# One attention output norm per query block, the residual sum on GpSimd, and shorter one-column roots in a two-layer hybrid decoder step

## The chip, the cores and the metric

The kernel runs on one core of a Trainium2 chip. The metric is device time in microseconds (us) from launch to end; the time of a kernel is the median of its runs. The engines are TensorE (PE in the profile; PEld is its weight load), VectorE (DVE), ScalarE (ACT), GpSimd (POOL) and SyncE (SP), whose queue issues the DMAs here. Each engine runs its own instructions in a fixed order; they wait for each other by semaphores.

## The reference, cut to what matters

One inference step of two layers over 2048 prompt tokens and 64 sample tokens (8 rows of 8), width 1024. Each layer projects its modulated input into four branches: A (differential attention), B (spatial gate), C (convolution), D (gated recurrence). Each branch is multiplied by a SiLU gate, the four are joined and projected, and the residual update normalizes the result:

```python
p = probs(q1, k1) - lam * probs(q2, k2)          # softmax over the visible keys
o_a = einsum('bhqk,bkhd->bqhd', p, v)            # 4 heads of 64 value columns
o_a = _rms_norm(o_a, attn_norm_g[l]) * (1.0 - lam_init)
o_a = o_a * silu(ag)
mixed = concatenate([o_a, o_b, o_c, o_d], -1) @ w_out[l]
y = _layer_norm(ALPHA * x + gate[:, None, :] * mixed, ln_g[l], ln_b[l])
```

`_rms_norm` divides the 64 values of a head by the root of their mean square plus EPS; `_layer_norm` takes the mean and the variance (plus EPS) of a row of 1024. ALPHA is (2 x 2 layers)^0.25.

## The kernel before

A layer has two stages. The first makes the projections and the branches B, C and D and writes queries, keys, values, gates and the joined branches to DRAM. The second, the attention stage, runs `attention` and `out_tile` (lines 1489 to 1516) and is the one that the change touches. In the profile it lies at 1065 to 1640 us for the first layer and at 2590 us to the end for the second.

The attention works on query blocks of tiles of 128 tokens: blocks of 4, 4, 4, 2 and 2 tiles, so 5 per layer. For each block, `attention` (line 620) loops over the 4 heads: it loads the head's keys and queries, and for each tile `attn_probs` (line 653) makes the scores on TensorE into one of two PSUM buffers (L668), the negated row maximum on VectorE (L672), the exponential on ScalarE with its row sum (L676), and joins the two softmaxes without dividing by the sum of the first (L697, L702; small columns in L674 to L692). `attn_value` (line 705) transposes the probabilities (L715, L717) and multiplies with the values (L720) into one PSUM bank. The row sum l of the first softmax stays in the tile `ls`.

After the last tile of a head, `attn_value` goes on with the norm of that head (lines 726 to 747): copy out of PSUM, transpose, copy to `ot`, square (ScalarE), sum of squares over 64 columns (L737), mean square plus EPS times l squared (L738, L739, since the output is not divided by l), the root (L740, which calls `rsqrt`, line 174: L179 and L181 for the first estimate, then three Newton steps in L183, L189 and L190), the product with the root (L742) and the product with the norm's weights (L746 on GpSimd; L744 on VectorE in the last block). The head's 64 columns are then stored to the scratch tensor `cat`, except in the last block, where they stay in `act`. `rsqrt` runs on VectorE here: its `pool` argument is false. Each step is one instruction on columns as wide as the number of tiles (4 or 2).

`out_tile` (line 1313) makes one tile of 128 tokens of the layer's output: it loads `cat`, the gates and the other branches, multiplies (L1336 on GpSimd, L1342 on VectorE), splits the product in a high and a low part (L110 on ScalarE, L172 mostly on GpSimd), multiplies with the two parts of `w_out` in two halves of 512 columns (L1360 to L1362), and for each half multiplies by the adaLN gate (L1364), adds ALPHA times the old x (L1365) and takes the statistics (L1366), all on VectorE. Then come mean and variance (L1368), EPS (L1370), the one-column root (L1371), the affine step on ScalarE (L1376) and the two products and sums with the LayerNorm's weights (L1377, L1378), on GpSimd except in the last two tiles, and the store. The output tiles of a block are emitted after the attention of the next block; the last two tiles (`last`) follow their own block directly. With the sample there are 17 tiles per layer. x and the gated product share four buffers (tag `xs`).

The order of the work on each engine is not the order of the code. A planner arranges the instructions before the run from a simulated timeline and from priorities (`prio`, offsets in `KN`: the output tiles have -500, the probabilities 0), and SP's queue has the loads and stores in one order as well. On the chip that order is fixed. Buffers are tiles of pools: a tile with `bufs=1` can be written again only after all its readers are done.

Of the kernel before, what the change touches and what calls it, by code (L numbers as in the profile page):

```python
# [9 lines left out]
F32 = mybir.dt.float32  # L10
# [4 lines left out]
AF = mybir.ActivationFunctionType  # L15
# [9 lines left out]
P = 128  # L25
# [43 lines left out]
def hymba_step_kernel(  # L69
# [21 lines left out]
    # order, engines and buffers: P* offsets of priority, E* / L* / R* choice of engine, the others counts and orders  # L91
# [16 lines left out]
    def cpy(k, out, in_):  # L108
        """copy by ScalarE or VectorE"""
        (nc.vector.tensor_copy if KN[k] else nc.scalar.copy)(out, in_)  # L110
# [18 lines left out]
    # pools of the phase: PSUM banks of the projections, a second bank for transposes  # L129
# [4 lines left out]
    def nm(s):  # L134
        uid[0] += 1
        return f"{s}_{uid[0]}"
# [14 lines left out]
    def st(tag, dt=F32):  # L151
        """rows of 512 of the streams that run beside each other: zs slabs, ms branches, os input and output"""
        return stp.tile([P, 512], dt, tag=tag, name=nm(tag), bufs=NST[tag])

    # small columns: width by stream
    SW = dict(d=8, a=4, b=2, c=4, o=1, s=4, p=4)
# [17 lines left out]
    def rsqrt(v, M, n, who, pool=True):  # L174
        """1 / sqrt(v) in place for v [M, n] > 0: estimate from the exponent bits, three Newton steps."""
# [5 lines left out]
        eng.tensor_scalar(y.bitcast(I32), i, -1.0, float(0x5F3759DF), op0=ALU.mult, op1=ALU.add)  # L181
        for _ in range(3):
# [10 lines left out]
    def gate2(dst, t, x):  # L193
        """2 silu(x) = (tanh(x / 2) + 1) x, given t = tanh(x / 2)"""
        nc.vector.scalar_tensor_tensor(dst, t, 1.0, x, op0=ALU.add, op1=ALU.mult)  # L195

# [16 lines left out]
    # page indices: row = (layer * NPOOL + page) * 128 + partition  # L213
# [15 lines left out]
    # conditioning vectors, transposed  # L229
# [50 lines left out]
    def mod(l, Lx, part, mp, bank=None):  # L280
        """shift, 1 + scale or gate of the rows of c, features on partitions."""
        dst = (Lx.shT, Lx.sc1T, Lx.gT)[part]
        for half in range(2):
# [7 lines left out]
            # the four sums are added once features are on partitions  # L291
# [14 lines left out]
        if part == 2:  # L306
            for half in range(2):
# [4 lines left out]
                nc.vector.tensor_copy(row[0:9], ps[0:9])  # L312
                store(scr[l].gate[:, half * 512:(half + 1) * 512], row[0:9])

    def prep(l, Lx, hp):
        """small tensors of a layer; hp: those that only the first phase needs"""
# [19 lines left out]
        with tc.tile_pool(name=nm("prep"), reuse_waits="tile", bufs=1) as pp:  # L336
# [16 lines left out]
            # lower bound: cumulative softmax over the layers, without the first  # L353
# [18 lines left out]
            # head norms; A and D carry the 1/2 of their gate  # L372
# [4 lines left out]
            # lambda of the differential attention  # L377
# [11 lines left out]
            # convolution taps  # L389
# [7 lines left out]
            # 1/4: the halves of the swish and of the gate  # L397
# [3 lines left out]
            # spatial weights, lower triangle  # L401
# [10 lines left out]
            # 1/2 of the gate in the weights and in the bias  # L412
# [13 lines left out]
    # state kept between the groups of a layer  # L426
# [92 lines left out]
    def tok_pairs(g):  # L519
        """(first token column, global tile, number of tiles, rows, is sample)"""  # L520
# [23 lines left out]
    def mix(main, n, *fills):  # L544
        """main (about n steps) with each fill (generator, steps, share of main over which it is spread) in between"""
# [18 lines left out]
    # ================= A: differential attention =================  # L564
# [55 lines left out]
    def attention(l, t0, nt, Lx, ap, act=None):  # L620
        """nt tiles of queries from tile t0"""
# [8 lines left out]
        vst = pool.vst  # L630
        for hd in range(4):
# [11 lines left out]
            ls = smp.tile([P, 4], F32, tag="ls", name=nm("ls"), bufs=3)  # L643
            acc = None
            for j in range(nt):
                pm = prio(KN['PPB'] if t0 else KN['PPB'], attn_probs, t0 + j, qt[:, :, j * P:(j + 1) * P], kst, ls[:, j:j + 1], Lx, ap)
# [3 lines left out]
                prev = (lambda *a: lambda: attn_value(*a, Lx, l, ap))(t0 + j, pm, vst, acc, ls, j, nt, hd, act)  # L650
        prev()

    def attn_probs(qi, qt, kst, l1, Lx, ap):
        """p1 - lam (l1 / l2) p2, unnormalized; l1"""
# [6 lines left out]
        for m in range(2):  # L661
            pms = []
            for pc, n in enumerate(sizes):
# [7 lines left out]
                # negated running maximum  # L671
# [7 lines left out]
            if npc > 1:  # L679
                # factor of the first part, whose maximum may have been smaller  # L680
# [24 lines left out]
    def attn_value(qi, pm, vst, acc, ls, j4, nt, hd, act, Lx, l, ap):  # L705
        """values of even key tiles on the lower columns of the array, of odd ones on the upper"""
# [19 lines left out]
        asb = ap.o.tile([P, 512], F32, tag="asb", name=nm("asb"), bufs=1)  # L726
        cpy('EAS', asb[:, 0:nt * P], acc[:, 0:nt * P])
        # transposed, the two halves of the columns added
# [3 lines left out]
        ot = ap.o.tile([P, 4, 64], F32, tag="ot", name=nm("ot"), bufs=1)[:, 0:nt]  # L732
        nc.scalar.copy(ot, pt[:, 0:nt * 64].rearrange("p (a v) -> p a v", v=64))
        sq = st("ms")[:, 0:nt * 64].rearrange("p (a b) -> p a b", b=64)
        nc.scalar.activation(sq, ot, AF.Square)
        ss, l2, lt = sm("a")[:, 0:nt], sm("a")[:, 0:nt], ls[:, 0:nt]
        nc.vector.tensor_reduce(ss, sq, AX.X, ALU.add)  # L737
# [824 lines left out]
```

## Time and profile before

| | us |
|---|---|
| median of 3 runs | 3179.31 |
| lowest and highest run | 3175.09, 3195.48 |
| profiled execution: span from its first to its last instruction | 3202.3 |
| attention stage of the first layer | 575.0 |
| attention stage of the second layer, to the end | 612.3 |

The profile is of one execution; no time is recorded for it beside its span. Busy time is the time in which at least one instruction of an engine is in work; the rows by line give the sum over a line's instructions, which can overlap by a little, and their mean. "idle before" is the time in which the engine stood still before an instruction, with what it waited for. A wait is put down to the releaser that came last.

### The profile page before, as it was taken

The page shows a single profiled execution, that of the slowest core. Times are in us where ns is not written, and L with a number is a line of the kernel's source. Part 1 is how long each engine was busy: PE and PEld are TensorE (multiplying, and loading weights), DVE is VectorE, ACT ScalarE, POOL GpSimd, SP SyncE. Part 2 cuts the span into 40 slices and gives each one's busy share as a digit, 9 for nine tenths or more (in the row PEclk, how much of TensorE's full clock was granted, in tenths as well). Part 3 has the DMA queues.
Part 4 walks back from the last instruction along what each step waited for, and adds up shares of the span by engine and source line. Part 5 has one row for each costly group of instructions (what it writes and reads, how often), then busy time and mean ns, then how long its engine had stood idle before and what let it go on. Part 6 is the DMA issues. An engine that isn't in the chain of part 4 may idle for free. (4 is left out here: it accounts for less than half of the span.)

```text
span 3202.3 us, 56179 instructions
## 1 busy us (share of the span) xinstructions
PE 2881.2 (90%) x20888; PEld 2260.0 (71%) x20888; DVE 2280.8 (71%) x5280; ACT 1223.5 (38%) x2564; POOL 1122.6 (35%) x1173
## 2 busy tenths in 40 slices
PE   6998999898999889979879989998989888997997
PEld 4888876688864466657668878776888656765665
DVE  3666883377692599988866667833776938998897
ACT  3111223312211466676642112233122137667663
POOL 4334455333230323412343443554342431241232
PEclk9999999899999899989989999998999998998998
DMA  6122323223324754546441222232232254544652
GB/s 224 61 72 85 90 83 119 79 64 93 111 90 154 192 148 129 142 103 162 122 149 57 74 88 87 86 120 81 64 105 88 69 152 120 132 130 110 150 154 72
DMA packets 343747, 353.26 MB, mean 110 GB/s; under 512 B 59728, under 2 KB 249718, under 8 KB 343459
## 3 DMA queue, kind: packets, MB, share of 16 engines
q1 hardware_dynamic: 337330, 332.90, 36.6%
q0 software_dynamic: 6144, 16.79, 1.8%
q8 instruction: 165, 2.70, 0.4%
q14 instruction: 108, 0.88, 0.1%
HBM read 266.44 MB, written 83.33 MB: 109 GB/s over the span
## 5 line engine op out<-in xcount | busy, mean ns | idle before, releaser
L515 PE MATMUL z<-hh,wh 128*128 128x512 f32 (+1 forms) x1440 | 526.5, 366 | 20.9 <-DVE zs L195 19.1
L172 POOL TENSOR_TENSOR wl<-raw,wh 128x512 fp32r<-128x512 f32 x224 | 323.1, 1455 | 609.1 <-ACT wh L110 562.8
L517 PE MATMUL z<-hh,wl 128*128 128x512 f32 (+1 forms) x1440 | 520.1, 362 | 0.0
L516 PE MATMUL z<-hl,wh 128*128 128x512 f32 (+1 forms) x1440 | 519.0, 361 | 0.0
L506 PE MATMUL z<-wh,hh 128*128 128x256 f32 (+1 forms) x1360 | 399.2, 294 | 12.6 <-issue 4.4
L1013 DVE SCALAR_TENSOR_TENSOR acc<-glu,cw,acc 128x512 f32<-128x512 f32 x480 | 402.2, 885 | 3.2
L507 PE MATMUL z<-wl,hh 128*128 128x256 f32 (+1 forms) x1360 | 394.8, 290 | 5.9 <-issue 5.9
L676 ACT ACTIVATE P<-S,stt 128x1024 f32<-128x1024 f32 (+7 forms) x384 | 332.9, 868 | 174.3 <-DVE stt L672 124.6
L508 PE MATMUL z<-wh,hl 128*128 128x256 f32 (+1 forms) x1360 | 395.7, 291 | 3.8 <-issue 3.6
L672 DVE TENSOR_REDUCE stt<-S 128x1 f32<-128x1024 f32 (+7 forms) x384 | 344.7, 905 | 62.1 <-PE S L670 45.1
L515 PEld LDWEIGHTS z<-hh,wh 128*128 128x128 f32 x1440 | 274.1, 190 | 81.7 <-DVE zs L195 23.5
L517 PEld LDWEIGHTS z<-hh,wl 128*128 128x128 f32 x1440 | 273.9, 190 | 50.9 <-issue 12.2
L516 PEld LDWEIGHTS z<-hl,wh 128*128 128x128 f32 x1440 | 274.0, 190 | 49.5 <-issue 13.8
L110 ACT CAST wh<-raw 128x512 fp32r<-128x512 f32 x224 | 133.8, 619 | 420.4 <-DMA raw<-in_w_in_dram 279.3
L668 PE MATMUL S<-K,Q 128*128 128x512 f32 (+3 forms) x640 | 226.8, 429 | 64.2 <-ACT P L676 53.6
L506 PEld LDWEIGHTS z<-wh,hh 128*128 128x128 f32 (+1 forms) x1360 | 262.0, 193 | 23.5 <-issue 10.0
L507 PEld LDWEIGHTS z<-wl,hh 128*128 128x128 f32 (+1 forms) x1360 | 261.8, 193 | 9.3 <-issue 7.8
L508 PEld LDWEIGHTS z<-wh,hl 128*128 128x128 f32 (+1 forms) x1360 | 261.9, 193 | 7.5 <-issue 5.2
L1360 PE MATMUL z<-woh,zs 128*128 128x512 f32 (+1 forms) x480 | 200.4, 417 | 16.1 <-ACT zs L110 10.1
L715 PE MATMUL T<-cst,P 128*128 128x128 f32 x1088 | 189.6, 303 | 25.1 <-DVE P L697 19.6
L172 POOL TENSOR_TENSOR zs<-os,zs 128x512 fp32r<-128x512 f32 (+1 forms) x64 | 84.3, 1319 | 348.0 <-ACT zs L110 339.1
L720 PE MATMUL X<-ph,V 128*64 128x128 f32 x2176 | 198.3, 296 | 8.1 <-ACT ph L717 7.6
(374 smaller groups left out, 5649.0 us busy)
## 6 DMA issues: line engine op xcount, KB each, us to landing
raw<-in_w_in_dram SPq DMA_DIRECT2D x128, 256.0 KB
K<-kh SPq DMA_DIRECT2D x224, 128.0 KB
K<-kl SPq DMA_DIRECT2D x224, 128.0 KB
mw<-in_w_ada_dram SPq DMA_DIRECT2D x96, 256.0 KB
raw<-in_w_in_dram SPq DMA_DIRECT2D x192, 128.0 KB
os<-gat SPq DMA_DIRECT2D x64, 256.0 KB
gat<-zs SPq DMA_DIRECT2D x48, 256.0 KB
os<-in_x_prompt_dram SPq DMA_DIRECT2D x32, 256.0 KB
```

Of the source, the lines that this page charges most:

```text
L172: eng.tensor_tensor(out, x, hi.bitcast(F32), ALU.subtract)
L506: nc.tensor.matmul(ps, hh[:, k, tok:tok + M], wh[:, k, :], start=(k == 0), stop=False)
L507: nc.tensor.matmul(ps, hh[:, k, tok:tok + M], wl[:, k, :], start=False, stop=False)
L508: nc.tensor.matmul(ps, hl[:, k, tok:tok + M], wh[:, k, :], start=False, stop=(k == KT - 1))
L515: nc.tensor.matmul(ps, wh[:, k, ms], hh[:, k, c0:c0 + n], start=(k == 0), stop=False)
L516: nc.tensor.matmul(ps, wh[:, k, ms], hl[:, k, c0:c0 + n], start=False, stop=False)
L517: nc.tensor.matmul(ps, wl[:, k, ms], hh[:, k, c0:c0 + n], start=False, stop=(k == KT - 1))
L668: nc.tensor.matmul(s[:, o:o + w], qt[:, m, :], kst[pc * 2 + o // 512][:, m, 0:w], start=True, stop=not diag)
L672: nc.vector.tensor_reduce(col(m, pc), s[:, :n], AX.X, ALU.max, negate=True)
L676: nc.scalar.activation(p[:, :n], s[:, :n], AF.Exp, bias=col(m, pc), scale=1.0, accum_out=l1 if m == 0 and npc == 1 else col(m, 2 + pc))
L1013: nc.vector.scalar_tensor_tensor(av, src(j), Lx.cw[:, c, j:j + 1], av, op0=ALU.mult, op1=ALU.add)
L1360: nc.tensor.matmul(po[0:M], a, wh[:, k, :], start=(i == 0), stop=False)
```

## The change

The norm of the attention's output moves out of `attn_value` to the end of `attention`: the four heads of a block are collected in one tile `ot` of 4 x 256 columns and their row sums in one `ls`, and square, sum, root and products are done once for all heads, on up to 16 columns. The square is cut in pieces of 512 columns. The product with the norm's weights is one GpSimd instruction per block (VectorE in the last block), in place, and there is one store per block. `asb` moves to the stream tag `ms`; the separate `act` goes. `rsqrt` gets a form for one column on VectorE: two Newton steps of two instructions each, whose constant factors are carried on, and a last step of three. In `out_tile` the residual sum becomes a plain sum on GpSimd (on VectorE in the last two tiles): the gate rows are divided by ALPHA when they are stored, and EPS by ALPHA squared.

```diff
-    SW = dict(d=8, a=4, b=2, c=4, o=1, s=4, p=4)
+    SW = dict(d=8, a=16, b=2, c=4, o=1, s=4, p=4)
...
     def rsqrt(v, M, n, who, pool=True):
...
         eng.tensor_scalar(y.bitcast(I32), i, -1.0, float(0x5F3759DF), op0=ALU.mult, op1=ALU.add)
+        if n == 1 and not pool:
+            c = 1.0
+            for _ in range(2):
+                eng.tensor_scalar(a, y, y, v, op0=ALU.mult, op1=ALU.mult)
+                eng.scalar_tensor_tensor(y, a, -3.0 * c * c, y, op0=ALU.add, op1=ALU.mult)
+                c = -2.0 * c ** 3
+            eng.tensor_scalar(a, y, y, v, op0=ALU.mult, op1=ALU.mult)
+            eng.tensor_scalar(a, a, -0.5 / c ** 3, 1.5 / c, op0=ALU.mult, op1=ALU.add)
+            eng.tensor_tensor(y, y, a, ALU.mult)
+            return y
...
-                nc.vector.tensor_copy(row[0:9], ps[0:9])
+                nc.vector.tensor_scalar(row[0:9], ps[0:9], 1.0 / ALPHA, None, op0=ALU.mult)
...
-    def attention(l, t0, nt, Lx, ap, act=None):
+    def attention(l, t0, nt, Lx, ap, last=False):
...
+        ls = smp.tile([P, 4, 4], F32, tag="ls", name=nm("ls"), bufs=2)
+        ot = ap.o.tile([P, 4, 256], F32, tag="ot", name=nm("ot"), bufs=1)
         for hd in range(4):
...
-            ls = smp.tile([P, 4], F32, tag="ls", name=nm("ls"), bufs=3)
...
-                prev = (lambda *a: lambda: attn_value(*a, Lx, l, ap))(t0 + j, pm, vst, acc, ls, j, nt, hd, act)
+                prev = (lambda *a: lambda: attn_value(*a, ap))(t0 + j, pm, vst, acc, ot, j, nt, hd)
         prev()
+        W = nt * 256
+        otf = ot.rearrange("p t c -> p (t c)")
+        q4 = lambda x: x.rearrange("p (a v) -> p a v", v=64)
+        ss, l2, lt = sm("a")[:, 0:nt * 4], sm("a")[:, 0:nt * 4], ls.rearrange("p t h -> p (t h)")[:, 0:nt * 4]
+        for c in range(0, W, 512):
+            n = min(512, W - c)
+            sq = st("ms")[:, 0:n]
+            nc.scalar.activation(sq, otf[:, c:c + n], AF.Square)
+            nc.vector.tensor_reduce(ss[:, c // 64:(c + n) // 64], q4(sq), AX.X, ALU.add)
+        nc.vector.scalar_tensor_tensor(l2, lt, EPS, lt, op0=ALU.mult, op1=ALU.mult)
+        nc.vector.scalar_tensor_tensor(ss, ss, 1.0 / 64.0, l2, op0=ALU.mult, op1=ALU.add)
+        ss = rsqrt(ss, P, nt * 4, "a", KN["RA"] and not last)
+        o4 = q4(otf[:, 0:W])
+        nc.vector.tensor_tensor(o4, o4, ss.unsqueeze(2).to_broadcast([P, nt * 4, 64]), ALU.mult)
+        (nc.vector if last else nc.gpsimd).tensor_tensor(o4, o4, Lx.ag.unsqueeze(1).to_broadcast([P, nt * 4, 64]), ALU.mult)
+        if not last:
+            store(tok_rows(scr[l].cat, t0, nt)[:, 0:256].rearrange("(t p) c -> p t c", p=P), ot[:, 0:nt])
+        return ot
...
-        asb = ap.o.tile([P, 512], F32, tag="asb", name=nm("asb"), bufs=1)
+        asb = st("ms")
...
-        ot = ap.o.tile([P, 4, 64], F32, tag="ot", name=nm("ot"), bufs=1)[:, 0:nt]
-        nc.scalar.copy(ot, pt[:, 0:nt * 64].rearrange("p (a v) -> p a v", v=64))
-        sq = st("ms")[:, 0:nt * 64].rearrange("p (a b) -> p a b", b=64)
...
-        store(tok_rows(scr[l].cat, qi - nt + 1, nt)[:, hd * 64:(hd + 1) * 64].rearrange("(t p) c -> p t c", p=P), on3)
+        nc.scalar.copy(ot[:, 0:nt, hs], pt[:, 0:nt * 64].rearrange("p (a v) -> p a v", v=64))
...
-            nc.vector.scalar_tensor_tensor(xt[0:M], xt[0:M], ALPHA, t[0:M], op0=ALU.mult, op1=ALU.add)
+            (nc.vector if last else nc.gpsimd).tensor_tensor(xt[0:M], xt[0:M], t[0:M], ALU.add)
...
-        nc.vector.tensor_scalar(rstd, mv[0:M, 1:2], EPS, None, op0=ALU.add)
+        nc.vector.tensor_scalar(rstd, mv[0:M, 1:2], EPS / ALPHA ** 2, None, op0=ALU.add)
...
-                act = op.tile([P, qb[1], 256], F32, name=nm("act")) if i == len(qbs) - 1 else None
...
-                prio(KN['PATT'], attention, l, *qb, Lx, ap, act)
+                act = prio(KN['PATT'], attention, l, *qb, Lx, ap, i == len(qbs) - 1)
```

## Rows read from the trace of the kernel before

**Rows 1.** Head of the page, and VectorE busy in tenths by slice.
```profile
span 3202.3 us, 56179 instructions
...
DVE  3666883377692599988866667833776938998897
```

**Rows 2.** Stretches: length, PE, PEld, DVE, ACT, POOL busy (count), clock, DMA.
```profile
1065.00:1640.00 575.00, 498.76 (x3076) 359.50 (x3076) 500.27 (x1245) 368.20 (x792) 183.92 (x149) 0.93 0.55 144
2590.00:3202.30 612.30, 526.71 (x3175) 375.43 (x3174) 510.40 (x1283) 371.17 (x793) 169.84 (x134) 0.93 0.49 129
1200.00:1360.00 160.00, 149.15 (x907) 109.03 (x906) 155.17 (x367) 103.30 (x222) 65.61 (x50) 1.00 0.50 135
2740.00:2900.00 160.00, 151.06 (x899) 109.92 (x896) 154.84 (x374) 104.54 (x222) 64.62 (x51) 0.99 0.51 134
1360.00:1440.00 80.00, 59.13 (x387) 41.82 (x386) 65.02 (x170) 61.25 (x132) 7.87 (x8) 0.83 0.43 103
```

**Rows 3.** Timeline at the end: start us, us, engine, line.
```profile
3173.33 0.39 PE L1361 MATMUL S<-wol,zs 128*128 128x512 f32 x1
...
3173.55 0.40 PE L1362 MATMUL S<-woh,zs 128*128 128x512 f32 x1
```

**Rows 4.** Waits, first attention stage: us in total, times, longest.
```profile
PE S L668 <- ACT P L676: 33.5, 31, 4.0
...
PE S L668 <- DMA K<-kl: 4.7, 3, 1.8
...
SPq L169 <- POOL ms L746: 29.2, 12, 4.3
```

**Rows 5.** Newton steps of the norm (tile smaa), VectorE, both stages.
```profile
sum 1187.30, DVE 84.02; mean DVE 42.01
```

**Rows 6.** Groups by line: count, busy us, mean ns, idle before.
```profile
L1378 POOL TENSOR_TENSOR x<-x,lnb 128x512 f32<-128x512 f32 (+1 forms) x60 | 78.9, 1334 | 0.0
...
L1365 DVE SCALAR_TENSOR_TENSOR x<-x,t 128x512 f32<-128x512 f32 (+1 forms) x68 | 47.7, 702 | 0.5
...
L674 DVE TENSOR_TENSOR stt<-stt 128x1 f32<-128x1 f32 x128 | 39.3, 307 | 0.4
...
L746 POOL TENSOR_TENSOR ms<-ms,ag 128x256 f32<-128x256 f32 (+1 forms) x32 | 23.5, 735 | 209.0 <-DVE ms L742 191.2 <-ACT P L676 11.7 <-DVE stt L687 2.4
...
L742 DVE TENSOR_TENSOR ms<-ot,smay 128x256 f32<-128x256 f32 (+1 forms) x40 | 16.1, 402 | 0.9
...
L737 DVE TENSOR_REDUCE sma<-ms 128x4 f32<-128x256 f32 (+1 forms) x40 | 14.2, 355 | 5.6 <-ACT ms L735 5.4
...
L1193 DVE TENSOR_REDUCE smd<-ms 128x8 f32<-128x512 f32 (+1 forms) x20 | 11.7, 587 | 5.4 <-ACT ms L1191 5.0
...
L181 DVE TENSOR_SCALAR smay<-smai 128x4 int32<-128x4 int32 (+1 forms) x40 | 11.7, 293 | 0.6
...
L179 DVE TENSOR_SCALAR smai<-sma 128x4 int32<-128x4 int32 (+1 forms) x40 | 11.2, 280 | 0.4
...
L739 DVE SCALAR_TENSOR_TENSOR sma<-sma,sma 128x4 f32<-128x4 f32 (+1 forms) x40 | 11.0, 274 | 0.1
...
L1197 DVE TENSOR_TENSOR ms<-T,smdy 128x512 f32<-128x512 f32 x16 | 11.0, 685 | 10.5 <-POOL smdy L187 10.4
...
L738 DVE SCALAR_TENSOR_TENSOR sma<-ls 128x4 f32<-128x4 f32 (+1 forms) x40 | 9.3, 232 | 0.0
```

**Rows 7.** Spread inside a line: count, duration ns min/median/max.
```profile
L189 DVE SCALAR_TENSOR_TENSOR smaa<-smaa,smay x120: 138/159/1257, 1099.0 to 3165.1; 128x4 f32<-128x4 f32 x72, 128x2 f32<-128x2 f32 x48
...
L697 DVE SCALAR_TENSOR_TENSOR P<-P,stt,P x64: 1269/1280/2294, 1224.2 to 3151.2; 128x1024 f32<-128x1024 f32 x64
...
L674 DVE TENSOR_TENSOR stt<-stt x128: 142/154/1246, 1213.8 to 3147.0; 128x1 f32<-128x1 f32 x128
```

**Rows 8.** Timeline in a mixed stretch: start us, us, engine, line.
```profile
1278.92 1.84 POOL L1377 TENSOR_TENSOR x<-x,lng 128x512 f32<-128x512 f32 x1 [3.81 <-ACT x L1376]
...
1279.53 1.25 DVE L189 SCALAR_TENSOR_TENSOR smaa<-smaa,smay 128x4 f32<-128x4 f32 x1
```

More of the change, by code (lines that the diff above doesn't have):

```diff
@@ L642, in attention @@
                 load(qt[q * 32:(q + 1) * 32, :, 0:nt * P], S.qs[gq][part][rows, oq:oq + nt * P].rearrange("(m d) t -> d m t", m=2))
-            ls = smp.tile([P, 4], F32, tag="ls", name=nm("ls"), bufs=3)
             acc = None
             for j in range(nt):
-                pm = prio(KN['PPB'] if t0 else KN['PPB'], attn_probs, t0 + j, qt[:, :, j * P:(j + 1) * P], kst, ls[:, j:j + 1], Lx, ap)
+                pm = prio(KN['PPB'] if t0 else KN['PPB'], attn_probs, t0 + j, qt[:, :, j * P:(j + 1) * P], kst, ls[:, j, hd:hd + 1], Lx, ap)
                 if prev is not None:
@@ L703, in attn_probs, with attn_value @@
         return p1s
-    def attn_value(qi, pm, vst, acc, ls, j4, nt, hd, act, Lx, l, ap):
+    def attn_value(qi, pm, vst, acc, ot, j4, nt, hd, ap):
         nk = qi + 1
@@ L731, in attn_value @@
             nc.tensor.matmul(pt[:, j * 64:(j + 1) * 64], asb[:, j * P:(j + 1) * P], diagm, start=True, stop=True)
-        ot = ap.o.tile([P, 4, 64], F32, tag="ot", name=nm("ot"), bufs=1)[:, 0:nt]
-        nc.scalar.copy(ot, pt[:, 0:nt * 64].rearrange("p (a v) -> p a v", v=64))
-        sq = st("ms")[:, 0:nt * 64].rearrange("p (a b) -> p a b", b=64)
-        nc.scalar.activation(sq, ot, AF.Square)
-        ss, l2, lt = sm("a")[:, 0:nt], sm("a")[:, 0:nt], ls[:, 0:nt]
-        nc.vector.tensor_reduce(ss, sq, AX.X, ALU.add)
-        nc.vector.scalar_tensor_tensor(l2, lt, EPS, lt, op0=ALU.mult, op1=ALU.mult)
-        nc.vector.scalar_tensor_tensor(ss, ss, 1.0 / 64.0, l2, op0=ALU.mult, op1=ALU.add)
-        ss = rsqrt(ss, P, nt, "a", KN["RA"] and act is None)
-        on3 = st("ms")[:, 0:nt * 64].rearrange("p (a b) -> p a b", b=64)
-        nc.vector.tensor_tensor(on3, ot, ss.unsqueeze(2).to_broadcast([P, nt, 64]), ALU.mult)
-        if act is not None:
-            nc.vector.tensor_tensor(act[:, :, hs], on3, Lx.ag.unsqueeze(1).to_broadcast([P, nt, 64]), ALU.mult)
-            return
-        pick('EAN').tensor_tensor(on3, on3, Lx.ag.unsqueeze(1).to_broadcast([P, nt, 64]), ALU.mult)
-        store(tok_rows(scr[l].cat, qi - nt + 1, nt)[:, hd * 64:(hd + 1) * 64].rearrange("(t p) c -> p t c", p=P), on3)
+        nc.scalar.copy(ot[:, 0:nt, hs], pt[:, 0:nt * 64].rearrange("p (a v) -> p a v", v=64))
     def attention_sample(l, Lx, Sx, ap):
```

## The prediction

> **What bounds the kernel now.** I read the page's slices first, then the stretches, then the waits, then the groups by line and the spread inside a line. The changed code runs almost only in the attention stage of each layer, and the page's VectorE slices place it: slices 15 to 17, 35, 36 and 39 (counting from 1) show 9, that is 90% busy or more, and most of the others of the stages 8 [rows 1]. The stretches say it closer: the two stages take 575.0 and 612.3 us, VectorE is busy for 500.27 and 510.40 of them, and in 1200 to 1360 and 2740 to 2900 us, where output tiles run beside the attention, for 155.17 and 154.84 of 160 us, that is 97%. TensorE shows 149.15 and 151.06 there, ScalarE two thirds, GpSimd 40% [rows 2]. TensorE's number is the softer one: matmuls of one line follow each other after 0.22 us while each is drawn 0.39 us long [rows 3], so its busy time holds some room that VectorE's does not. In 1360 to 1440 us no output tile runs; VectorE is busy 65.02 of 80 us, ScalarE 61.25, and the clock granted to TensorE is 0.83 [rows 2]: there the chain scores, maximum, exponential sets the pace. The waits agree: TensorE's longest in the first stage is for the exponentials (33.5 us in 31 waits: the next scores want a PSUM buffer back), while key loads cost it 4.7 us [rows 4]. So VectorE bounds the mixed stretches (about 540 us of the two stages by the slices), and a chain bounds the rest, where VectorE is one of three members.
>
> **Part 1, the norm.** Removed: 40 chains (4 heads, 5 query blocks, 2 layers) of 15 VectorE instructions. The nine Newton steps take 84.0 us [rows 5]; the reduction, the two columns of the sum and EPS, the two of the estimate and the multiply take 14.2 + 9.3 + 11.0 + 11.2 + 11.7 + 16.1 = 73.5 us [rows 6]. Together 157.5 us. Added: 10 chains, one per block. Their reductions are 16 of 512 columns at 0.587 us = 9.4 (the nearest row is the same reduction of another branch [rows 6]). Their 13 column instructions cost 10 x 13 x 0.16 = 20.8 us, with 0.159 the median of such a step [rows 7]; 16 columns instead of 4 are no length at this price. Their multiplies are 6 of 1024 columns at 1.28 (the median of the same size in the probabilities [rows 7]) and 4 of 512 at 0.70 = 10.5. That is 40.7, so -117 us. But the removed steps hold waits that may not leave: a Newton step takes 84.02 / 360 = 0.233 us in the mean and 0.159 in the median, up to 1.257 [rows 5, 7]. At 1278.92 a GpSimd multiply starts, and the VectorE step issued at 1279.53 takes 1.25 us and ends with it [rows 8]. These waits are 360 x 0.074 = 27 us, and 160 x 0.11 = 17 in the other column instructions (mean 0.27). If the same waits fall on other instructions, the gain is 117 - 44 = 73. I take -95, half way. On GpSimd 32 multiplies by the norm's weights (23.5 us [rows 6]) become 8 larger ones, about 18 us by their columns.
>
> What hides the rest: the chain now stands at the end of a block and is longer (square, two reductions, 13 columns, one wide multiply, a wide GpSimd multiply, one store), some 10 us. Its only readers before the last block are the output tiles, which run one block later. The output buffer is single: the next block's first head must not copy before the store has landed. A stage holds 20 heads, so one lasts 575.0 / 20 = 29 us in the mean [rows 2], and 10 us are covered even at half of that; without that cover each of the 8 hand-overs costs up to 10 us, and the bound is +80 us. I take 0. The store moves too: 32 stores become 8 on SP's queue, where the stores wait for GpSimd 29.2 us in 12 waits in the first stage, with key loads queued behind [rows 4]; since key loads hardly stop TensorE, I count nothing. At the end of each layer the last head's chain is exposed and gets wider, by about 0.3 + 0.3 + 0.4 + 0.4 us (reduction and multiplies of 512 instead of 128 columns, and the square): +3 us for both.
>
> **Part 2, the residual sum.** 60 sums leave VectorE: 60 x 0.702 = 42.1 us [rows 6]. 60 go to GpSimd at 1.334 us, its price for a sum of that size [rows 6]: +80 us on 353.8 us of GpSimd [rows 2], less the 5 above. What does GpSimd's time cost VectorE? The lower end is nothing. A first count is the 44 us of waits in part 1; the minimum of the two maxima adds (0.307 - 0.154) x 128 = 20 us [rows 6, 7]. These 648 instructions are a quarter of VectorE's 2528 in the stages [rows 2] and carry 64 us, 0.18 us per us of GpSimd; other instructions with inputs in SBUF wait as well (a 1024-column one has a median of 1.280 and a maximum of 2.294 [rows 7]). Twice that, 0.4, is my value: +75 x 0.4 = +30 us; the far end is 1.0, +75.
> By the Trainium skill ("SBUF — State Buffer", section "SBUF: two separate sides") GpSimd and a VectorE instruction with two inputs in SBUF share one port pair under an exclusive lock, and whoever starts first keeps it for the whole instruction. The row at 1279.53 agrees with that rule; by it the full 75 us could come back, as in rival A. The median of 0.159 us says that most VectorE instructions do not meet it.
>
> The sum also adds a wait: the statistics follow it on VectorE, in a fixed order, and the softmax maxima of later tiles are queued behind them; the exponentials and so the scores wait for those. In the kernel before, the multiply of the D branch waits in this way for GpSimd's root: 10.5 us in 16 [rows 6], 0.65 each. So 60 x 0.65 = 39 us if that held here, 0 if other work is put between. I take +10. Part 2 is then -42 + 30 + 10 = -2, between -42 and +72.
>
> **Part 3, the roots.** 34 LayerNorm roots have 9 column instructions instead of 11: 34 x 2 x 0.16 = -11 us. Their new form with two column operands does not stand in the trace; the near end is the same price, the far end is three of them at double price, 34 x 3 x 0.16 = 16, so +5. I take -8. The constants folded into the gate rows and EPS cost nothing: the copy becomes a scaled copy.
>
> **The sum.** VectorE -95 - 2 - 8 = -105 us of 1011, about a tenth. In the mixed stretches (540 of 1187 us) a microsecond less on VectorE is nearly one less; in the others it shortens one member of the chain of three. I take one half overall: -53, and +3 for the ends: -50 us. The profiled execution spans 3202.3 us [rows 1]; 3202.3 - 50 = 3152 is 1.56% less. That execution lies 23 us above the median of the runs, so I apply the share to the median: 3179 x 0.9844 = 3130 us. The likeliest case's own range is 3080 (-120 us at 0.85, +3: 3202.3 - 99) to 3150 (-65 us at one half). All terms at their lower ends are -117 - 42 - 11 = -170 us, at 0.8 about 3047 us, and all at their upper ends -73 + 72 + 5 = +4, about 3185 us; a missing cover of the single buffer would come on top, and its +80 us lies outside the range.
>
> **The rivals.**
> A, the port: every GpSimd microsecond more lands on VectorE. Part 2 is then -42 + 75 + 10 = +43, the total -60, half of it -30, with the ends -27: 3152 us. For it: the step that ended with GpSimd's multiply. Against: the medians. Chance 0.17.
> B, the gain stays where nothing waits: TensorE's 149 of 160 us are real, or the order of the queues falls out worse, and a fifth of the 105 us arrives: -21 + 3 = -18, 3161 us. For it: the busy numbers. Against: matmuls 0.39 us long following after 0.22. Chance 0.13.
> C, slower, by the new wait: GpSimd works in pairs; the first multiply of 1278.92 took 1.84 us. If each sum queues behind one such instruction and then takes 1.33, each statistic holds VectorE for 1.84 + 1.33 - 0.3 = 2.9 us (0.3 for a short instruction or two in between): 60 x 2.9 = 172 us where I took 10. VectorE's total is then -105 + 162 = +57; standing time counts about 0.6: +34 + 3, 3216 us. It turns from gain to loss where the mean wait passes (105 + 10) / 60 = 1.9 us. For it: the fixed order, and GpSimd's pairs. Against: in the D branch the same kind of wait was 0.65. Chance 0.13.
>
> **How the numbers follow.** The forecast has 0.57, A 0.17, B 0.13, C 0.13. One per cent, 32 us, is about what a measurement of this kernel can tell from no change. Faster by over 1% (below 3147): nearly all of the forecast (0.52) and two fifths of A (0.07), 0.59. Slower by over 1% (above 3211): most of C and a little of the spread of B, 0.12. Within: 0.29. The range goes from 3080 to 3190: it holds the forecast, A and B, and leaves out C and a tail below.
>
> **What would show it.** Right: the norm's chain is there 10 times, VectorE's busy time in the two stages falls by 70 to 110 us, and each stage gets shorter by 15 to 40 us. TensorE's wait for the exponentials is next late. GpSimd rises to about 430 us in the stages. Part 2 shows as VectorE idle before the statistics, released by GpSimd: up to 20 us keeps the forecast, over 110 is C. Medians of column steps at 0.16 with a mean above 0.25 speak for A. Wrong: VectorE's busy time falls as said while the stages keep their length (B), or the first head of a block waits for the store of the block before. Outside the attention stages nothing should move by more than a few us.

## The result, and the profile after

The changed kernel takes 3202.72 us (median of 12 runs, 3195.06 to 3214.08) against 3183.47 us for the kernel before on the same chip (12 runs): ratio 1.0056, 95% interval 1.004 to 1.0071, some 18 us more. The forecast was 50 us less. It lies outside the range, on the other side.

Against that of after, the profiled execution of before is about 20 us longer outside the attention stages: its first score starts 9.6 us later, and 10.7 us more lie between its two stages (marks below). So spans are not compared here; stages and busy totals are. The page of after: head, busy totals, VectorE's slices.

```profile
span 3199.5 us, 55497 instructions
...
PE 2877.8 (90%) x20888; PEld 2259.3 (71%) x20888; DVE 2221.0 (69%) x4694; ACT 1218.5 (38%) x2540; POOL 1197.9 (37%) x1209
...
DVE  3667873377782688878966678733767848888786
```

The same line of totals of the page of before:

```profile
PE 2881.2 (90%) x20888; PEld 2260.0 (71%) x20888; DVE 2280.8 (71%) x5280; ACT 1223.5 (38%) x2564; POOL 1122.6 (35%) x1173
```

VectorE has 586 instructions and 59.8 us less, GpSimd 75.3 us more, TensorE and ScalarE are as they were. No slice of the stages shows 9 any more on VectorE but one (in [rows 1] there were six). The stretches of after, columns as in [rows 2]:

```profile
1065.00:1640.00 575.00, 497.27 (x3063) 357.86 (x3063) 466.80 (x949) 360.61 (x769) 219.04 (x162) 0.93 0.53 140
2590.00:3199.50 609.50, 515.49 (x3111) 369.12 (x3109) 477.84 (x986) 365.66 (x777) 207.69 (x151) 0.91 0.46 126
1200.00:1360.00 160.00, 144.45 (x888) 106.44 (x887) 134.33 (x289) 103.04 (x220) 71.95 (x55) 0.97 0.42 119
2740.00:2900.00 160.00, 144.78 (x891) 108.15 (x890) 135.71 (x286) 102.39 (x224) 74.81 (x55) 0.94 0.45 124
```

In the mixed stretches VectorE went from 97% to 84%, and nothing took its place: TensorE fell as well (149.15 to 144.45, 151.06 to 144.78), and the clock granted to it from 1.00 and 0.99 to 0.97 and 0.94. The stages are longer all the same. Score matmuls (L668, in after L701) and value matmuls (L720, in after L753), each stage on its own, before and then after; first and last start stand behind the durations:

```profile
L668 PE MATMUL S<-K,Q x320: 218/397/797, 1069.9 to 1593.6; 128*128 128x512 f32 x136, 128*128 128x128 f32 x8, 128*128 128x256 f32 x8, 128*128 128x384 f32 x8
...
L720 PE MATMUL X<-ph,V x1088: 272/273/477, 1077.7 to 1616.6; 128*64 128x128 f32 x182
...
L668 PE MATMUL S<-K,Q x320: 218/397/797, 2623.1 to 3143.9; 128*128 128x512 f32 x136, 128*128 128x128 f32 x8, 128*128 128x256 f32 x8, 128*128 128x384 f32 x8
...
L720 PE MATMUL X<-ph,V x1088: 272/273/477, 2638.4 to 3158.5; 128*64 128x128 f32 x182
```

```profile
L701 PE MATMUL S<-K,Q x320: 218/398/796, 1060.3 to 1596.7; 128*128 128x512 f32 x136, 128*128 128x128 f32 x8, 128*128 128x256 f32 x8, 128*128 128x384 f32 x8
...
L753 PE MATMUL X<-ph,V x1088: 272/273/476, 1067.6 to 1612.3; 128*64 128x128 f32 x182
...
L701 PE MATMUL S<-K,Q x320: 220/398/796, 2608.1 to 3138.3; 128*128 128x512 f32 x136, 128*128 128x128 f32 x8, 128*128 128x256 f32 x8, 128*128 128x384 f32 x8
...
L753 PE MATMUL X<-ph,V x1088: 272/273/476, 2624.6 to 3156.0; 128*64 128x128 f32 x182
```

From the first score to the last value, before takes 546.7 and 535.4 us and after 552.0 and 547.9. The difference, 5 + 13 = 18 us, is as large as the whole loss, so by these two executions the loss sits in the attention stages.

Where VectorE's time went shows in groups that the change doesn't touch. First before, then after (L702 is now L735, L697 L730, L688 L721, L683 L716):

```profile
L702 DVE SCALAR_TENSOR_TENSOR P<-P,stt,P 128x128 f32<-128x128 f32 (+7 forms) x128 | 111.3, 869 | 0.5
...
L697 DVE SCALAR_TENSOR_TENSOR P<-P,stt,P 128x1024 f32<-128x1024 f32 x64 | 86.4, 1349 | 6.4 <-ACT P L696 5.8
...
L688 DVE SCALAR_TENSOR_TENSOR stt<-ls,nlam,stt 128x1 f32<-128x1 f32 x128 | 42.1, 329 | 0.8
...
L683 DVE SCALAR_TENSOR_TENSOR stt<-stt 128x1 f32<-128x1 f32 x64 | 22.8, 356 | 8.5 <-ACT stt L681 8.3
...
L683 DVE SCALAR_TENSOR_TENSOR ls<-stt 128x1 f32<-128x1 f32 x64 | 13.5, 211 | 1.0 <-ACT stt L681 1.0
```

```profile
L735 DVE SCALAR_TENSOR_TENSOR P<-P,stt,P 128x128 f32<-128x128 f32 (+7 forms) x128 | 129.4, 1011 | 1.3
...
L730 DVE SCALAR_TENSOR_TENSOR P<-P,stt,P 128x1024 f32<-128x1024 f32 x64 | 92.7, 1449 | 3.6 <-ACT P L729 3.5
...
L721 DVE SCALAR_TENSOR_TENSOR stt<-ls,nlam,stt 128x1 f32<-128x1 f32 x128 | 52.3, 409 | 2.2
...
L1384 DVE BATCH_NORM_STATS2 obs<-x 128x6 f32<-128x512 f32 (+1 forms) x68 | 46.5, 683 | 6.5 <-POOL x L1383 6.4
...
L716 DVE SCALAR_TENSOR_TENSOR stt<-stt 128x1 f32<-128x1 f32 x64 | 31.9, 498 | 27.0 <-ACT stt L714 26.5
...
L716 DVE SCALAR_TENSOR_TENSOR ls<-stt 128x1 f32<-128x1 f32 x64 | 28.7, 449 | 13.0 <-ACT stt L714 10.9 <-ACT P L709 2.0
```

The same instructions on the same sizes cost 18.1 + 6.3 + 10.2 + 9.1 + 15.2 = 58.9 us more, as much as VectorE lost in all (59.8), and others wait longer for ScalarE. Much of this growth belongs to the order of the queues and not to the work. The five groups take 276.1 us in before and 335.0 in after, but 303.7 and 302.1 in the two other orders of the same work below, and 286.4 in a kernel of the same order and the same VectorE work as before, with fewer matmuls. So of the 58.9 us, 26 to 28 come with the work in other orders too, some 10 of them no more than two totals differ by anyway, and about 31 come with this order alone. L1384 is rival C's place: the statistics wait 6.4 us for GpSimd, not 172.

### The profile page after: what moved, and what is told of

It is laid out like the page before. It is cut to its first block, busy times and chain, and to the rows that moved or that the text cites. A ratio compares the mean times of both kernels' runs of the same rounds, so it can differ in the third digit from the quotient of the medians.

```text
span 3199.5 us, 55497 instructions
## 1 busy us (share of the span) xinstructions
PE 2877.8 (90%) x20888; PEld 2259.3 (71%) x20888; DVE 2221.0 (69%) x4694; ACT 1218.5 (38%) x2540; POOL 1197.9 (37%) x1209
## 4 chain that ended last, share of the span: by engine, by line
PE 49%; DVE 34%; DMA 5%; ACT 4%; issue 4%; POOL 2%; SPq 1%; DVEq 0%; ACTq 0%; POOLq 0%
DVE acc L1031 10%; PE z L527 5%; PE z L529 5%; PE z L528 5%; DVE stt L705 5%; PE z L518 3%; PE z L519 3%; PE z L520 3%; PE T L748 3%; PE X L753 3%; PE S L701 2%; ACT P L709 2%; DVE P L735 2%; PE z L1378 2%; PE z L1380 2%
## 5 line engine op out<-in xcount | busy, mean ns | idle before, releaser
L518 PE MATMUL z<-wh,hh 128*128 128x256 f32 (+1 forms) x1360 | 398.7, 293 | 11.4 <-ACT zs L487 4.7
L701 PE MATMUL S<-K,Q 128*128 128x512 f32 (+3 forms) x640 | 231.0, 436 | 76.4 <-ACT P L709 67.6
L1378 PE MATMUL z<-woh,zs 128*128 128x512 f32 (+1 forms) x480 | 200.7, 418 | 18.3 <-ACT zs L110 9.3
L753 PE MATMUL X<-ph,V 128*64 128x128 f32 x2176 | 199.7, 298 | 12.5 <-ACT ph L750 11.6
L750 ACT COPY ph<-T 128x512 f32<-128x512 f32 (+2 forms) x320 | 160.3, 524 | 116.2 <-PE T L748 115.1
```

Of the source, the lines that this page charges most:

```text
L518: nc.tensor.matmul(ps, hh[:, k, tok:tok + M], wh[:, k, :], start=(k == 0), stop=False)
L701: nc.tensor.matmul(s[:, o:o + w], qt[:, m, :], kst[pc * 2 + o // 512][:, m, 0:w], start=True, stop=not diag)
L753: nc.tensor.matmul(acc[e * 64:(e + 1) * 64, j4 * P:(j4 + 1) * P], vst[c // 4][:, j, hs], ph[:, j, :], start=(c + j < 2), stop=(c + j >= nk ...
```

## The experiments

All times are ratios to the kernel before on the same chip in the same job. Its median went from 3184 to 3209 us between jobs, which had different chips, so times of different jobs aren't compared.

**Each part alone.** The change minus the root and the sum; before plus the sum; before plus the root; the change with its sum on VectorE:

```diff
-            (nc.vector if last else nc.gpsimd).tensor_tensor(xt[0:M], xt[0:M], t[0:M], ALU.add)
+            nc.vector.tensor_tensor(xt[0:M], xt[0:M], t[0:M], ALU.add)
```

> The norm per block alone; roots and residual sum as before. Theory G (the 60 sums on GpSimd hold VectorE's softmax columns and eat the gain): without them the norm's saving shows, 20 to 50 us under the kernel before. Rival N (the norm at the end of the block, or the order of the queues that it brings, costs more than it saves): 10 to 25 us over the kernel before, as the whole change. Rival R (the new root does the harm): as theory G.

> The residual sum on GpSimd alone; norm and roots as before. Theory G: slower than before by 25 us or more, since the sums cost more than the 42 us that leave VectorE give. Rival N: the same as before within 10 us, or faster. Rival R: the same as before.

> The shorter one-column root alone. Theory G and rival N: within 8 us of the kernel before. Rival R: slower by 10 us or more, since two-column operands cost more than the instructions that go.

> The whole change, but with the residual sum on VectorE (a plain sum). Theory G: 25 to 55 us under the kernel before. Rival N: 5 to 30 us over it. Rival R: over it, while the norm alone is under it.

Measured: norm 1.0061 (1.0037 to 1.0085), sum 1.0001 (0.998 to 1.0021), root 1.0100 (1.0065 to 1.0135), norm and root 1.0051 (1.0028 to 1.0073). The sum is neither gain nor loss. But a root with 76 column steps less can't well cost 30 us by its work, and norm and root together cost less than the root alone. What these kernels share is that each has its own order of the queues from the planner.

**The same work in another order.** From here on many kernels hold the order of each engine's queue. The instructions of an engine are chained in a listed order; such a link (declared `NoSync`) is to order the issue and add no wait:

```diff
     with _tile.TileContext(nc, **TCK) as tc:
         hymba_step_kernel(tc, *args)
+        hold(nc, tc)
...
+    for n in np.cumsum(d):
+        i = names.get("I-%d" % n)
...
+        if i.engine in last:
+            tc.add_manual_dep(i, last[i.engine].name, info, reason="order")
+        last[i.engine] = i
```

The list is another kernel's order; instructions that it doesn't have stand where those that they replace stood. Where that order can't be (a buffer would be written before it is read), an instruction is moved back as far as needed; where it was counted, the expectations say how many.

> The short root alone, but every engine's queue is held in the order of the kernel before (what is common stands in the same place; seven column steps stand where nine stood). With its own order the short root took 3217.9 us, 1.0100 of the kernel before. Theory O (the planner's new order of the queues costs the time, not the work): 0.995 to 1.002 of before, since 76 column steps of 0.24 to 0.27 us leave VectorE and nothing else changes. Theory W (the work itself: a longer dependent chain in the root, or the freed VectorE time moving waits): 1.007 to 1.013, as with its own order.

> The work of the kernel before (three Newton steps with nine column steps), but every queue held in the order that the planner made for the short root. Theory O: 1.007 to 1.014 of before, as the short root itself in that order. Theory W: 0.998 to 1.003, since the work is that of the kernel before.

> The whole change (norm per block, sum on GpSimd, short root), but every queue held as near to the order of the kernel before as its dependences allow: the norm of a block stands where the norm of its last head stood, the sum on GpSimd where VectorE's stood; of VectorE's 4694 instructions 10 and of TensorE's 16964 231 stand elsewhere, most of them at the end of a layer. With its own order the change took 1.0056 of before. Theory O: 0.984 to 0.998 of before (the predicted gain of 50 us or part of it comes back). Theory W: 1.003 to 1.010.

> The work of the kernel before, but every queue held in the order of the changed kernel: the norms of the first three heads, which that kernel doesn't have, stand right where the head's result is copied. Theory O: 1.008 to 1.025 of before (the changed kernel's 1.0056, and the VectorE work that it saved on top of it). Theory W: 0.998 to 1.004.

Measured: root in the old order 1.0013 (0.9993 to 1.0033); before in the root's order 1.0105 (1.0085 to 1.0125). The short root costs nothing, and neither do the links that hold the order; its own order costs 1%. The whole change in the old order 1.0116 (1.0095 to 1.0137), so for the rest of the change theory O fell: the old order doesn't bring the gain back. Before in the changed kernel's order 1.0438 (1.0417 to 1.0458): an order fits the work it was made for. So a loss in a borrowed order can be the work or the misfit; one wait that is plainly misfit is found below.

**A new order and nothing else.** One priority, on the kernel before and on the changed one:

```diff
-              POUT=-500, PATT=0, PMOD=0, PW=0, PAV=0, PDZ=3000, PQK=500, PSL=0, PSLD=0, PPR=0, PPB=0, OT=1, GO=0, DO=0,
+              POUT=-500, PATT=0, PMOD=0, PW=0, PAV=-50, PDZ=3000, PQK=500, PSL=0, PSLD=0, PPR=0, PPB=0, OT=1, GO=0, DO=0,
```

> The kernel before with no work changed: only the priority of the value step is set 50 lower, so that the planner lays the queues out in another order (nothing is held). Theory O (a new order alone is worth as much as the whole change): off by 0.3 to 1.5 per cent, more likely slower than faster. Otherwise: within 0.3 per cent.

> The changed kernel with no work changed, only the priority of the value step 50 lower (nothing held): a second order of its queues from the same planner. Theory O: off from the changed kernel's 1.0056 by 0.3 to 1.5 per cent on either side, so 0.991 to 1.021 of before. Otherwise 1.003 to 1.009.

Measured: 1.0106 (1.008 to 1.0131) on the kernel before, 0.9985 (0.9968 to 1.0002) on the changed one, whose own order gave 1.0056. With no work changed, the order is worth 1.1% on the one, for the worse, and 0.7% on the other, for the better. VectorE's total moves with it. The changed kernel at the new priority:

```profile
PE 2888.0 (90%) x20888; PEld 2265.6 (71%) x20888; DVE 2184.0 (68%) x4694; ACT 1220.3 (38%) x2540; POOL 1196.3 (37%) x1209
```

The same 4694 instructions take VectorE 2221.0 us in the change's own order, 2196.3 in the old one and 2184.0 here. At the new priority nearly the 105 us of the forecast left VectorE (96.8), and the kernel is still only level with before.

**What is scarce in the attention stages.** In the order of before: TensorE's second product left out (L1361), GpSimd's last gain and bias left out (L1377, L1378), and the same two put on VectorE.

```diff
-                nc.tensor.matmul(po[0:M], a, wl[:, k, :], start=False, stop=False)
...
-            (nc.vector if last or not KN['GP'] else nc.gpsimd).tensor_tensor(r, r, O.g[0:M, js], ALU.mult)
-            (nc.vector if last else nc.gpsimd).tensor_tensor(r, r, O.b[0:M, js], ALU.add)
+            nc.vector.tensor_tensor(r, r, O.g[0:M, js], ALU.mult)
+            nc.vector.tensor_tensor(r, r, O.b[0:M, js], ALU.add)
```

> The kernel before in its own order of the queues, without the second of the three products of the output projection (activations by the low part of the weights): 544 fewer TensorE matmuls of 0.39 us, about 107 us of TensorE's busy time less in each attention stage; VectorE, ScalarE and GpSimd do all they did. Theory T (TensorE's queue paces the attention stages, which is why VectorE time taken away at the same order gave nothing): 0.935 to 0.975 of before. Theory L (the round from a score tile over VectorE's maximum and ScalarE's exponential back to the score buffer paces them): 0.985 to 1.003.

> The kernel before in its own order of the queues, without the last gain and bias of the output tiles on GpSimd (120 operations of 1.3 to 1.5 us, 166 of GpSimd's 364 us in the two stages). GpSimd then holds VectorE up for some 65 to 80 us less in all. Theory P (what GpSimd takes from VectorE is on the path): 0.98 to 0.992. Theory T or L (VectorE is not what paces the stage): 0.995 to 1.002.

> The kernel before in its own order (45 of ScalarE's, 43 of VectorE's and 185 of TensorE's instructions elsewhere), with the last gain and bias of the output tiles on VectorE in place of GpSimd: 166 us less on GpSimd, 120 operations of some 0.68 us, 82 us, more on VectorE, which is busy 86 per cent of these stages. Leaving the two out gave 0.9886. If VectorE's own time costs nothing and GpSimd's does (it is the blocking and the longer way of a tile that is paid): 0.987 to 0.996. If VectorE's time is paid by one half, as the prediction had it: 1.000 to 1.006. If it is paid in full: 1.01 to 1.02.

Totals without the second product, then without gain and bias, then with these two on VectorE:

```profile
PE 2811.0 (88%) x20344; PEld 2188.5 (68%) x20344; DVE 2292.2 (72%) x5280; ACT 1224.9 (38%) x2564; POOL 1109.7 (35%) x1173
```

```profile
PE 2870.4 (91%) x20888; PEld 2252.9 (72%) x20888; DVE 2210.1 (70%) x5280; ACT 1222.1 (39%) x2564; POOL 955.3 (30%) x1053
```

```profile
PE 2901.7 (90%) x20888; PEld 2269.0 (70%) x20888; DVE 2293.5 (71%) x5400; ACT 1225.0 (38%) x2564; POOL 958.1 (30%) x1053
```

Without the product 1.0003 (0.9984 to 1.0022): theory T fell. VectorE's total is 11.4 us above before here though its work and order are the same, so a difference of some 10 us between two totals shows little. Without gain and bias 0.9886 (0.9858 to 0.9915), 36 us: GpSimd has 167.3 us less, and VectorE, which executes the same 5280 instructions, 70.7 us less, 0.42 us for each of GpSimd. That is one half of a microsecond for each of VectorE, if it is VectorE's time that was paid and not GpSimd's. With the two on VectorE 1.0036 (1.0019 to 1.0054). Between these two kernels GpSimd does the same, VectorE has 83.4 us more, and the kernel 1.5%, 48 us: 0.57 (0.44 to 0.71). So VectorE's busy time is still what counts here.

**The price of the block's end.** The norm alone in the order of before; the same with the last block's norm per head; the same with squares and sums per head; and before, with the norms of the first three heads left out in every block but the last of a layer, and nothing put at the end:

```diff
+        on3 = ot
+        if hd == 3 or act is not None:
-        sq = st("ms")[:, 0:nt * 64].rearrange("p (a b) -> p a b", b=64)
+            sq = st("ms")[:, 0:nt * 64].rearrange("p (a b) -> p a b", b=64)
...
```

> The norm per block alone, every queue held as near to the order of the kernel before as its dependences allow (244 of TensorE's and 19 of VectorE's instructions elsewhere). With its own order it took 1.0061. The whole change in the order of before took 1.0116; if that loss comes from the norm of the last block, which the last tiles' transposes and the next layer's first weights then wait for, this one is at 1.007 to 1.013; if it came from the sum on GpSimd, 0.995 to 1.003.

> The norm per block in the order of the kernel before (which took 1.0116), but in the last block of each layer (two tiles) the norm stays per head, in place, so that the last output tiles and the next layer's first weights wait for one head's norm and not for four. If the loss sits there (11 of its 20 us lay between the two attention stages): 0.997 to 1.006. If it comes from the other four blocks' norms, which come 10 to 20 us later than the first heads' did: 1.007 to 1.013.

> The norm per block in the order of before (1.0116), but the squares and their sums stay per head, at the head's place; at the block's end only the root, the multiplication, the gain and the store are left. VectorE does 24 small sums more. If the length of the chain at the block's end is what costs: 1.002 to 1.009. If it is something else (the single buffer, the later store of the block): 1.009 to 1.015.

> The kernel before in its own order of the queues (14 of TensorE's and 5 of VectorE's instructions elsewhere); the norms of the first three heads of every block but the last are left out (24 norms of 15 VectorE operations, some 90 us of VectorE's busy time in the two stages, and a square on ScalarE each), so that those heads get their gain alone. No norm at the block's end is put in their place. If freed VectorE time is worth one half, as the prediction had it: 0.982 to 0.989. If these operations stood in VectorE's queue where it would have waited anyway: 0.996 to 1.002, and then the 1.2 per cent of the norm per block in this order is the price of the block's end. If half is right, that price is 1.2 per cent and 45 us more.

Totals of the norm per block in the old order, and of the kernel with three norms left out:

```profile
PE 2879.5 (89%) x20888; PEld 2260.7 (70%) x20888; DVE 2235.1 (69%) x4830; ACT 1220.3 (38%) x2540; POOL 1113.7 (35%) x1149
```

```profile
PE 2879.8 (90%) x20888; PEld 2261.0 (71%) x20888; DVE 2225.6 (70%) x4920; ACT 1216.2 (38%) x2540; POOL 1122.7 (35%) x1173
```

Norm per block 1.0116 (1.0089 to 1.0143), the same as the whole change in this order. Three norms out 0.9941 (0.9918 to 0.9965): 19 us for 55.2 us of VectorE, a rate of 0.34 (0.2 to 0.5). The norm per block saves VectorE 45.7 us, worth 16 us at that rate, and is 37 us slower: some 53 us stand against it.

Part of them is the misfit. TensorE's waits for ScalarE's casts in 1600 to 1700 us, where the first layer ends (us in total, times, longest), in before and in the norm per block in the old order:

```profile
PE S L1360 <- ACT zs L110: 1.7, 2, 1.0
```

```profile
PE S L1367 <- ACT zs L110: 15.3, 2, 14.3
```

In ScalarE's queue a cast of the last output tile stands behind seven casts of the next layer's weights, which wait for their loads: the values to cast are ready at 1647.9 us, the cast starts at 1662.67, and TensorE stands still. All five kernels here that gather the norm and hold the old order have this one wait, 14.1 to 14.8 us long; in those that hold it with the norm per head the longest is 1.7 us, and the changed kernel and the norm alone, in their own orders, have none. From the first layer's last value matmul to the second's first score the norm per block takes 1006.2 us and the kernel without the second product, on the same chip, 995.1; the whole change in the old order 1017.0 and the root in it 1002.7. So 11 to 14 of the 37 us are a wait that holding the order made. About 40 us are left for the norm's place at the block's end (33 to 46 by the range of the rate). In its own order the norm alone comes to much the same: 19 us slower with 43.6 us less on VectorE, worth 15, makes 34. The whole change at the other priority, 5 us faster with 96.8 less, worth 33, makes 28. But an order alone moves the time by 20 to 35 us here, so none of the three is the price of the work by itself.

The two kernels that take the block's end apart leave most of it: last block per head 1.0089 (1.0072 to 1.0106), sums per head 1.0104 (1.0079 to 1.013), neither clearly different from 1.0116. So neither the squares and sums nor the last block are the main part; the last block can be 9 us, or none, or up to 19. What a row shows is the single output buffer. The copy into it, norm per block in the old order:

```profile
L754 ACT COPY ot<-T x40: 242/362/407, 1091.8 to 3177.3; 128x256 f32<-128x256 f32 x24, 128x128 f32<-128x128 f32 x16
...
  DMA cat<-ot: 5.4, 3
who waited for it (us, times):
  PEld T L737: 13.9, 6
  PE T L737: 12.5, 6
```

Three copies wait for the store of the block before, and TensorE's transposes stand 13 us behind copies; in before the same copy waited for no store and held the transposes for 1 us. That could be a third of the 40 us, but it was not tried alone, and it can't be what the block's end costs in every order: in the changed kernel's own order the copies wait 3.2 us for the store and the transposes 0.9 us for a copy, and in the norm alone in its own order there is neither wait. What the rest is stays open.

**Putting the saved time to use.**

> In the order of the kernel before: norm per block except in the last one, short root, residual sum on VectorE as before, gain and bias of the output tiles on VectorE. VectorE does about what it did before (some 90 us less and 82 us more), GpSimd 166 us less. If the saved VectorE time is what carries the moved work: 0.985 to 0.996, below both kernels. If the norm's block end costs its 1 per cent wherever it is: 0.998 to 1.01.

1.0116 (1.0095 to 1.0137): the loss is there as well, the misfit's one wait (14.8 us) with it. No kernel that does the whole work came out clearly below before; the best are the changed kernel with the other priority (0.9985) and the sum alone (1.0001).

## Why the prediction was wrong

- **What bounds.** Right in part. TensorE's busy time is soft, as [rows 3] said: 544 matmuls less changed nothing. VectorE's time counts, at 0.34 to 0.57.
- **The half.** It held, within what these runs can tell, where work was taken away in an unchanged order: 0.34 for the norms, 0.5 for GpSimd's blocking.
- **Part 1, VectorE's share.** Mis-sized: -95 was taken and -73 was the near bound; the norm alone gave -45.7 (old order) and -43.6 (own order, DVE 2237.2 on its page). Of the 117 us that were to go, 71 to 73 stayed or came back, where "the same waits fall on other instructions" had 44. At 0.34 the 43.6 are worth 15 us and not 48: about half of what the norm missed in its own order.
- **Part 1, the block's end. This is the step that failed.** "10 us are covered even at half of that ... I take 0", with +3 for the ends, came out at about 34 us in the norm's own order and 40 in the old one, the misfit's wait taken off; it is the other half of the miss. Each figure holds what its order is worth as well. The text had the sign and the size as an upper bound, "+80 us", and left it out of the range. But the mechanism that it priced, a copy that waits for the store, shows only 3 to 12 us of waits, or none. The cover was reckoned from a mean, 29 us for a head, and for that one reader only. These queues run in order and each waits for the others, so a chain of 10 us may cost without a late reader, by moving what stands behind it on VectorE, ScalarE and GpSimd. This last is argued; the runs show that a price of some 28 to 40 us is there in each order tried and leave its cause open.
- **Part 2.** Right: -2 expected, 1.0001 measured. VectorE 2259.8 against 2280.8 on its page, -21.0, where -42 + 30 = -12 was taken; the price of GpSimd, 0.4, measured 0.42 when two operations were taken away, (42.1 - 21.0) / 76.9 = 0.27 when one was added (0.13 more or less, with 10 us of doubt in a total). The wait was 6.4 us where 10 was taken. Rival C fell, and so did A: not all of GpSimd's time lands on VectorE. By the rule of the Trainium skill ("SBUF — State Buffer", section "SBUF: two separate sides") GpSimd and a VectorE instruction with two inputs in SBUF exclude each other at a shared port. The 0.42 agrees with it as a price for part of the time.
- **Part 3.** Work right, result wrong: -8 expected, VectorE 2275.9 (-4.9) in the old order and 1.0013. In its own order 1.0100.
- **The sum.** It had no term for the planner. "The order of the queues falls out worse" stood in rival B with 0.13 and no price beyond a lost gain; it is worth about 1%, more than the whole change. With what was measured: in the old order VectorE's -84.5 us (2196.3) at 0.34 gives -29, the block's end +40, the misfit's wait +13, together +24; measured +37, and its interval reaches down to 30, so some of it stays unexplained. The changed kernel's own order gives some 19 us of that back, which would be the wait and a little more, and the other priority some 42.
- **What would show it.** "Wrong: VectorE's busy time falls as said while the stages keep their length, or the first head of a block waits for the store". The first was seen, at 66 us in the two stages where 70 to 110 were said; the second hardly, with three copies and 3.2 us.

## What to carry to other kernels

Where a planner lays out in-order queues, an edit is two changes: the work and a new order. Time a change of priority alone first, and hold the old order to see what the work is worth; here the order moved the time by 1% and made a harmless root look like a loss. A held order that had to be bent brings waits of its own: search it for single long waits, at the seams between stages above all, before the loss is put down to the work. When small operations are gathered into one at the end of a block, price that end (one chain, one store, one buffer) within the range and not at nothing because its reader comes late.

## What was not expected of the hardware

TensorE gave back little when matmuls were taken out. At the 0.22 us by which they follow each other [rows 3], 544 are 120 us; its busy total fell by 70.2. The first stage without the second product, and two groups of both stages, in before and then without it:

```profile
1065.00:1640.00 575.00, 465.52 (x2794) 325.92 (x2793) 497.04 (x1236) 366.16 (x787) 180.67 (x146) 0.88 0.55 142
```

```profile
L720 PE MATMUL X<-ph,V 128*64 128x128 f32 x2176 | 198.3, 296 | 8.1 <-ACT ph L717 7.6
...
L715 PE MATMUL T<-cst,P 128*128 128x128 f32 x1088 | 189.6, 303 | 25.1 <-DVE P L697 19.6
```

```profile
L720 PE MATMUL X<-ph,V 128*64 128x128 f32 x2176 | 211.3, 310 | 12.2 <-ACT ph L717 11.0 <-DMA V<-v 0.8
...
L715 PE MATMUL T<-cst,P 128*128 128x128 f32 x1088 | 205.7, 323 | 46.2 <-DVE P L697 37.3 <-DVE smay L181 2.3 <-DVE smaa L183 1.8
```

The granted clock, a mean over the two levels of 1.2 and 2.4 GHz, was 0.88 where it was 0.93 [rows 2], with fewer matmuls in the same time, and the remaining ones took longer: 310 ns for 296 (L720) and 323 for 303 (L715) in before. Here a TensorE with more slack was also a slower one.
